# Filling each expected wait of TensorE without a break, and list-scheduling with instruction durations as profiled

## The chip, the cores and the metric

The kernel runs on one core of one Trainium2 chip. The metric is the device time in microseconds (us) of one launch; the time given is a median over runs. Five engines work side by side and each takes its instructions strictly in the order in which they were issued: TensorE (PE: matrix products, and transposes by a product with the identity), VectorE (DVE), ScalarE (ACT), GpSimd (POOL) and SyncE (SP, which issues DMAs). An engine whose next instruction waits for another engine stands still, whatever stands ready behind it. Products land in PSUM; this kernel has eight tiles of 128 x 512 fp32 values there, called banks below (`ps`), and DVE or ACT must read a bank out before it can be used again.

## The reference

The reference is a four-layer decoder on 512 tokens of width 1024, all in fp32. Each layer is a mixer and then a gated feed-forward layer (FFN, hidden width 2816), with RMS norms before each:

```python
def swiglu(x, w_in, w_out):
    gate, up = jnp.split(x @ w_in, 2, axis=-1)
    return (jax.nn.silu(gate) * up) @ w_out
...
    h = x
    for i in range(DEPTH):
        t, j = i % N_MIXERS, i // N_MIXERS
        hn = rmsnorm(h, norm_mix[i])
        if t == 0:
            m = rwkv7_mix(hn, ...)
        elif t == 1:
            m = swa_sink_mix(hn, ...)
        elif t == 2:
            m = sgu_chunk_mix(hn, ...)
        else:
            m = gla_mix(hn, ...)
        h = h + m
        h = h + swiglu(rmsnorm(h, norm_ffn[i]), ffn_w_in[i], ffn_w_out[i])
    return rmsnorm(h, norm_final)
```

The four mixers differ. RWKV-7 is a recurrence over tokens with a 64 x 64 state for each of 16 heads; sliding-window attention (SWA) has sinks and rotary positions; the gated spatial unit (SGU) mixes within chunks of 128 tokens; gated linear attention (GLA) is a recurrence over chunks of 64.

## The kernel before, in words

The kernel is written as a straight program of tile operations. Every operation is first recorded (the recorder is line 233, so nearly every instruction carries that line in the profile), with what it depends on. `Program.run` then is a list scheduler: it keeps a modelled clock for each engine, looks at a window of 700 recorded operations, takes the one that can start first by the model, and issues it. The order that it finds is fixed in the program; the chip only follows it. `Program.price` gives the model's two numbers for each operation: for how long it holds its engine, and how much later its result can be used by another one. For a DVE operation on n elements these are 68 + 1.042 n ns and 130 ns; for ACT 50 or 92 + 0.833 n ns and 150 ns.

Dense projections are done as three products of split operands (high and low parts, in the format fp32r), 512 columns each; the FFN uses a seven-product scheme whose weight combinations are added up by DMAs that POOL issues. ACT makes the high part of each weight tile (`whi<-wraw`), DVE the low part (`wlo<-wraw,whi`). The RWKV mixer is computed in chunks of 64 tokens: per group of four heads a preparation (`rwkv_prepare`, `rwkv_products`, `rwkv_inverse`, tiles `et`, `qk`, `pa`, `pr`, `mt`, `iv`) and then the chain over the chunks (`rwkv_chain`, tiles `wu`, `vu`, `st`, `tok`). Its products are small (64 or 128 columns) and depend on each other by way of DVE, ACT and POOL. An fp32 product of 128 columns appears in the trace as two records, a transpose or an fp32r product as one.

The scheduler also keeps TensorE at work while it has nothing to do. `K.__init__` records a product of the 128 x 128 identity (`ident`) with itself into a bank that nobody reads: line 453 in the profile of this kernel. Whenever TensorE's next operation starts later than the engine is free, `run` calls `keep_warm`. The kernel before divides time into stretches of half of 3413 ns (`PARTS`) and issues such unread products in each stretch only until a goal of work is reached (`LEVEL` x `BUSY` columns over the whole 3413 ns); the rest of the wait stays empty. An unread product takes the bank that has been free for longest, as any other would (`pool.slots["ps"].free`), and if the bank's last user was TensorE itself, the built product waits for TensorE's own semaphore.

Of the kernel before, what the change touches and what calls it, by code (L numbers as in the profile page):

```python
# [17 lines left out]
P = 128  # L18
# [8 lines left out]
PARTS = ((4, 5), (0, 1), (2, 3))  # L27
# [10 lines left out]
class View:  # L38
# [3 lines left out]
    def __init__(self, buf, dims, p0, lo, steps):  # L42
        self.buf, self.dims, self.p0, self.lo, self.steps = buf, dims, p0, lo, steps
# [146 lines left out]
class Program:  # L190
# [2 lines left out]


    WINDOW, SLACK, SEM = 700, 60.0, 100.0
    FREE, LEVEL, MARGIN, PARTS = 4, 1.0, 300.0, 2
    TICK, BUSY = 10240 / 3, 3350.0

    def __init__(self, tc):
        self.tc, self.ops, self.last = tc, [], None  # L200
        nc = tc.nc
        self.tensor, self.vector, self.scalar = Engine(self, "PE", nc.tensor), Engine(self, "DVE", nc.vector), Engine(self, "ACT", nc.scalar)
        self.gpsimd, self.sync = Engine(self, "POOL", nc.gpsimd), Engine(self, "SP", nc.sync)
        self.cold, self.warm, self.fills = 0.0, None, 0

    def pool(self, name, bufs, **kw):
        return Pool(self, name, bufs, kw)
# [54 lines left out]
    def price(self, eng, what, args, kw):  # L262

        views = [a for a in list(args) + list(kw.values()) if isinstance(a, View)]
        n = max(v.free() for v in views)
        columns = sum(v.free() == 1 and v is not views[0] and n > 1 for v in views)
        if what == "dma_start":
            return (490.0 if eng == "SP" else 1000.0), 2000.0
        if eng == "PE":
            if what == "transpose":  # L270
                return 109.0, 200.0
            m, n = args[1].free(), args[2].free()
            if args[2].dtype == F32R:
                return max(n * 0.4167 + 13.5, m * 0.83), 200.0
            return max(n * 1.667 + 5.0, m * 1.667, 340.0 if n < 16 and m == P else 0.0), 200.0
        if eng == "DVE":
            if what == "memset":
                return n * 1.05, 130.0
            fast = what in ("tensor_copy", "tensor_scalar") and not any(v.buf.psum for v in views)
            return 68.0 + n * (0.52 if fast else 1.042) + 61.0 * columns, 130.0  # L280
        if eng == "ACT":
            return (50.0 if any(v.buf.psum for v in views[1:]) else 92.0) + n * 0.833 + 94.0 * columns, 150.0
        if what == "tensor_copy":
            return 36.0 + n * 3.66, 130.0
        return 37.0 + n * (0.83 if len(views) < 3 else 2.8 if views[0].dims[-1][0] < 32 else 2.32), 130.0

    def run(self):
        ops, n = self.ops, len(self.ops)
# [10 lines left out]
        self.work, self.near = work, {}  # L299
        avail = {e: [] for e in now}  # L300
        head, limit = 0, 0
        order = 0
        while order < n:
# [8 lines left out]
            for e, lst in avail.items():  # L312
                cand, floor = None, None
                for i, op in lst:
                    s = max(now[e], op.ready)
                    ok = True
                    for b in op.bufs:
# [6 lines left out]
                        s = max(s, min(sl.free) + self.SEM)  # L324
# [18 lines left out]
            s, i, op, e = best  # L343
# [7 lines left out]
            cost = op.cost  # L351
            if e == "PE":
                tick = int(s // self.TICK)
                if work.get(tick - 1, 0.0) < self.BUSY:
                    self.cold += cost
                    cost *= 2
                self.count(work, self.TICK, s, cost, op.columns)
                self.count(self.near, self.TICK / self.PARTS, s, cost, op.columns)
            end = s + cost
            now[e] = end  # L360
            fin = end + op.lat
# [29 lines left out]
    def keep_warm(self, now, s, work):  # L391

        pool, call, first = self.warm
        t, free = max(now, s - 2 * self.TICK), pool.slots["ps"].free
        span = self.TICK / self.PARTS
        goal = self.LEVEL * self.BUSY / self.PARTS
        while first.done and free and min(free) + self.SEM <= t:
            n = int(t // span)  # L400
            done, end = self.near.get(n, 0.0), (n + 1) * span
            c = 218.0 if work.get(int(t // self.TICK) - 1, 0.0) >= self.BUSY else 436.0
            left = (end - t) / c * 512.0 - (goal - done)
# [10 lines left out]
            self.count(self.near, span, t, c, 512.0)  # L414
            t += c
            if t > s:
                return t
        return now

    def count(self, work, span, t, cost, columns):  # L420
        n = int(t // span)
# [1359 lines left out]
```

## Time and profile before

| | |
|---|---|
| median of three runs | 2632.45 us (2628.38 to 2634.78) |
| the profiled execution's own time | 2641.05 us |
| its span, first to last instruction | 2639.3 us |
| TensorE busy | 2554.7 us, 97%, 12974 records |
| DVE, ACT, POOL busy | 1853.8, 1331.6, 466.0 us |
| unread products, records in the trace | 320 (160 products) |
| mean granted TensorE clock | 0.982 |

The order of the stages in the span: the RWKV mixer up to about 575 us (its first projections up to about 150), then FFN 0, SWA (about 900 to 1100), FFN 1, SGU (about 1425 to 1725), FFN 2, GLA (about 2050 to 2300) and FFN 3. A busy TensorE need not be at its peak: products overlap in the pipeline, their ends are modelled, and gaps shorter than the last product's tail don't show as idle time.

### The profile page before, as it was taken

The numbers are of one execution on the slowest core, as the hardware profiler recorded it, in microseconds if no ns is written. First come the engines' busy times: TensorE is split into PE (matmuls) and PEld (weight loads), VectorE is DVE, ScalarE is ACT, GpSimd is POOL, SyncE is SP. The second block draws the span as 40 slices with busy tenths as digits, with TensorE's granted clock in tenths as the row PEclk, the third lists the DMA queues.
The fourth block names the chain that finished last, engine by engine and source line by source line (L and its number), as shares of the span: only waits on it lengthen the run. The fifth ranks groups of instructions, "written<-read, shape, count | busy, mean of one in ns | idle before, by whom it ended". The sixth has DMA issues, their size and how long they took to land.

```text
span 2639.3 us, 34990 instructions
## 1 busy us (share of the span) xinstructions
PE 2554.7 (97%) x12974; PEld 2083.4 (79%) x12974; DVE 1853.8 (70%) x2888; ACT 1331.6 (50%) x2208; POOL 466.0 (18%) x492
## 2 busy tenths in 40 slices
PE   8999889999999999999999999999999999999998
PEld 7667767889888775888787888898878777888886
DVE  8675777568787966676868474478777735577868
ACT  3544343356555655655555342365645633555545
POOL 1013333311212234121112000012121000012111
PEclk8989989999999999999999999999999999999999
DMA  3220001148988622499896222379897321389885
GB/s 126 72 68 9 7 7 37 39 126 219 226 215 213 178 84 50 101 223 229 208 227 185 96 96 88 80 176 224 211 228 170 119 96 50 81 221 223 209 209 125
DMA packets 127146, 366.24 MB, mean 139 GB/s; under 512 B 13424, under 2 KB 20976, under 8 KB 126976
## 3 DMA queue, kind: packets, MB, share of 16 engines
q0 software_dynamic: 41472, 138.43, 29.1%
q1 hardware_dynamic: 85504, 225.59, 25.3%
q8 instruction: 102, 1.67, 0.3%
q14 instruction: 68, 0.56, 0.1%
HBM read 359.51 MB, written 2.10 MB: 137 GB/s over the span
## 4 chain that ended last, share of the span: by engine, by line
PE 47%; DMA 5%; issue 5%; DVE 5%; ACT 2%; POOL 0%; SPq 0%; ACTq 0%; POOLq 0%; DVEq 0%
PE ps L233 47%; DMA wraw<-ffn_o_a 2%; DMA wraw<-ffn_w_b 2%; DVE slot L233 2%; DVE wlo L233 1%; ACT whi L233 1%; DVE left L233 1%; DMA wraw<-ffn_w_a 1%; ACT slot L233 1%; POOL wraw L233 0%; DVE h L233 0%; DVE mx L233 0%; DMA wraw<-ffn_o_b 0%; DMA slot<-sg_b_s 0%; DMA slot<-slot 0%
## 5 line engine op out<-in xcount | busy, mean ns | idle before, releaser
L233 PE MATMUL ps<-whi,slot 128*128 128x512 f32 (+1 forms) x5072 | 1548.3, 383 | 14.1 <-DVE slot L233 10.0
L233 PEld LDWEIGHTS ps<-whi,slot 128*128 128x128 f32 x5072 | 942.3, 188 | 190.2 <-issue 22.7
L233 DVE TENSOR_TENSOR wlo<-wraw,whi 128x1024 fp32r<-128x1024 f32 (+2 forms) x628 | 723.1, 1157 | 421.7 <-ACT whi L233 420.5
L233 ACT CAST whi<-wraw 128x1024 fp32r<-128x1024 f32 (+3 forms) x632 | 626.6, 995 | 695.5 <-PE ps L233 528.5
L233 PE MATMUL ps<-wlo,slot 128*128 128x512 f32 (+1 forms) x2536 | 969.3, 382 | 3.7 <-DVE wlo L233 3.6
L233 PEld LDWEIGHTS ps<-wlo,slot 128*128 128x128 f32 x2536 | 476.6, 188 | 87.4 <-DVE wlo L233 7.5
L233 PE MATMUL ps<-slot,whi 128*128 128x512 f32 (+2 forms) x864 | 275.0, 396 | 1.2 <-ACT slot L233 0.9
L233 POOL DMA_DIRECT2D wraw<-ffn_w_a x128 | 109.5, 857 | 502.7 <-DVE wlo L233 363.0
L233 DVE TENSOR_TENSOR slot<-ps,slot 128x512 f32<-128x512 f32 (+2 forms) x287 | 153.3, 566 | 60.4 <-PE ps L233 45.7
L233 PEld LDWEIGHTS ps<-slot,whi 128*128 128x128 f32 (+2 forms) x864 | 156.7, 184 | 48.6 <-issue 9.1
L233 POOL DMA_DIRECT2D wraw<-ffn_w_b x64 | 54.8, 864 | 744.6 <-DMA wraw<-ffn_w_b 505.8
L233 PE MATMUL ps<-slot,wlo 128*128 128x512 f32 (+2 forms) x432 | 169.7, 393 | 0.3 <-DVE wlo L233 0.3
L233 DVE TENSOR_TENSOR slot<-left,slot 128x512 fp32r<-128x512 f32 (+1 forms) x214 | 138.9, 666 | 34.9 <-ACT slot L233 29.1
L233 DVE TENSOR_TENSOR h<-h,ps 128x512 f32<-128x512 f32 x192 | 126.7, 682 | 26.4 <-PE ps L233 25.9
L233 ACT CAST slot<-left 128x512 fp32r<-128x512 f32 (+1 forms) x214 | 124.1, 606 | 31.8 <-PE ps L233 24.7
L233 POOL DMA_DIRECT2D wraw<-ffn_o_a x64 | 54.7, 854 | 278.4 <-DVE wlo L233 162.5
L233 ACT COPY slot<-ps 128x512 f32<-128x512 f32 (+2 forms) x137 | 76.1, 568 | 52.1 <-PE ps L233 51.8
L233 PEld LDWEIGHTS ps<-slot,wlo 128*128 128x128 f32 (+2 forms) x432 | 79.5, 184 | 21.2 <-DVE wlo L233 2.2
L233 PEld LDWEIGHTS ps<-ident,slot 128*128 128x128 f32 x580 | 68.3, 142 | 34.5 <-issue 9.5
L233 PE MATMUL ps<-ident,slot 128*128 128x128 f32 x580 | 89.6, 277 | 3.3 <-POOL slot L233 2.6
L233 ACT COPY left<-ps 128x512 f32<-128x512 f32 x100 | 50.6, 556 | 63.7 <-PE ps L233 63.7
L233 DVE TENSOR_TENSOR slot<-slot 128x512 fp32r<-128x512 f32 (+9 forms) x93 | 61.5, 666 | 18.5 <-ACT slot L233 17.1
(260 smaller groups left out, 2517.3 us busy)
## 6 DMA issues: line engine op xcount, KB each, us to landing
wraw<-ffn_w_a SPq DMA_DIRECT2D x128, 512.0 KB, 6.6
wraw<-ffn_w_a POOLq DMA_DIRECT2D x128, 512.0 KB, 6.0
wraw<-ffn_o_a SPq DMA_DIRECT2D x64, 512.0 KB, 4.8
wraw<-ffn_o_a POOLq DMA_DIRECT2D x64, 512.0 KB, 7.5
wraw<-ffn_w_b SPq DMA_DIRECT2D x64, 384.0 KB, 3.5
wraw<-ffn_w_b POOLq DMA_DIRECT2D x64, 384.0 KB, 6.5
wraw<-ffn_o_b SPq DMA_DIRECT2D x16, 512.0 KB, 5.5
wraw<-ffn_o_b POOLq DMA_DIRECT2D x16, 512.0 KB, 6.1
```

Of the source, the lines that this page charges most:

```text
L233: op = self.add(eng.name, lambda: getattr(eng.target, what)(*map(real, args), **{k: real(a) for k, a in kw.items()}), *self.price(eng.name ...
```

## The change

Three things change, all in the scheduler; what the kernel computes stays. First, `keep_warm`: where the model expects TensorE to wait for at least `GAP` = 450 ns, unread products are issued one behind the other until the next of them would end later than `TAIL` = 150 ns before the expected end of the wait. There is no goal any more. Second, `price`: the time for which DVE, ACT and POOL are held goes up (DVE 68 to 148 ns + 1.042 n, ACT 50 or 92 to 158 or 195 ns, POOL 36 or 37 to 60 ns), while the delay until the result can be used goes down (130 or 150 to 60 ns), so that the sum of the two hardly moves. A DVE scan now costs 2.1 ns an element in place of 1.042. Third, for TensorE an fp32 product costs 1.72 n in place of 1.667 n, and 0.56 of that where two products on 64 rows each follow each other on the two halves of the array.

```diff
-    FREE, LEVEL, MARGIN, PARTS = 4, 1.0, 300.0, 2
+    FREE, GAP, TAIL = 4, 450.0, 150.0
     TICK, BUSY = 10240 / 3, 3350.0
...
             if args[2].dtype == F32R:
                 return max(n * 0.4167 + 13.5, m * 0.83), 200.0
-            return max(n * 1.667 + 5.0, m * 1.667, 340.0 if n < 16 and m == P else 0.0), 200.0
+            return max(n * 1.72 + 5.0, m * 1.72, 340.0 if n < 16 and m == P else 0.0) * (0.56 if other else 1.0), 200.0
         if eng == "DVE":
...
-            return 68.0 + n * (0.52 if fast else 1.042) + 61.0 * columns, 130.0
+            return 148.0 + n * (0.52 if fast else 2.1 if what == "tensor_tensor_scan" else 1.042) + 61.0 * columns, 60.0
         if eng == "ACT":
-            return (50.0 if any(v.buf.psum for v in views[1:]) else 92.0) + n * 0.833 + 94.0 * columns, 150.0
+            return (158.0 if any(v.buf.psum for v in views[1:]) else 195.0) + n * 0.833 + 94.0 * columns, 60.0
...
     def keep_warm(self, now, s, work):
         pool, call, first = self.warm
-        t, free = max(now, s - 2 * self.TICK), pool.slots["ps"].free
-        span = self.TICK / self.PARTS
-        goal = self.LEVEL * self.BUSY / self.PARTS
-        while first.done and free and min(free) + self.SEM <= t:
...
-            if done > goal:
-                if end + c > s:
-                    break
-                t = end + 1.0
-                continue
-            if t + c > s and not 0.0 <= left < self.MARGIN:
-                break
+        free = pool.slots["ps"].free
+        if not first.done or not free or s - now < self.GAP:
+            return now
+        t = max(now, min(free) + self.SEM)
+        while True:
+            c = 224.0 if work.get(int(t // self.TICK) - 1, 0.0) >= self.BUSY else 448.0
+            if t + c > s - self.TAIL:
+                return now
             call()
...
             t += c
+            now = t
```

The built program holds 568 unread products in place of 160, in 104 groups in place of 61. 395 of them (145 before) stand ahead of FFN 0's first product, 62 of these (35 before) in the first four groups of the program, and 173 (15 before) behind FFN 0's beginning. Twelve groups have 13 products or more and hold 321 together. As the prices differ, the order of all other work moves as well: the lists of TensorE, DVE and ACT differ nearly everywhere in the RWKV mixer, and SP issues some of SWA's copies (`slot<-slot`) later among its weight loads.

TensorE, in the RWKV mixer, where a group's chain over the chunks (`wu`, `vu`) meets the next group's triangular blocks (`mt`, made by DVE and POOL), before:

```order
L233 MATMUL ps<-vu,tok 128x128 x2
L233 MATMUL ps<-vu,pr 64x64 x4
L233 MATMUL ps<-ident,h 128x128 x4
L233 MATMUL ps<-ident,et 128x128 x4
L453 MATMUL ps<-ident 128x128 x10
L233 MATMUL ps<-ident,mt 128x128 x4
L233 MATMUL ps<-mt,z 128x128 x4
L233 MATMUL ps<-st,qk 128x128
```

and now:

```order
L233 MATMUL ps<-vu,tok 128x128 x2
L233 MATMUL ps<-vu,pr 64x64 x4
L233 MATMUL ps<-ident,et 128x128 x4
L233 MATMUL ps<-ident,h 128x128 x4
L444 MATMUL ps<-ident 128x128 x62
L233 MATMUL ps<-ident,mt 128x128 x4
L233 MATMUL ps<-mt,z 128x128 x4
L233 MATMUL ps<-st,qk 128x128 x2
```

The group of ten unread products has become one of 62; the shorter groups that stood in the chain ahead of it are fewer.

TensorE, some 40 rows earlier in the same chain, where a chunk's solve (`wu,iv`) waits for ACT's copy of `wu`, now:

```order
L233 MATMUL ps<-wu,iv 64x64 x4
L233 MATMUL ps<-twa,wa 128x512
L233 MATMUL ps<-vu,pa 64x64 x4
L233 MATMUL ps<-vu,pr 64x64 x4
L444 MATMUL ps<-ident 128x128 x23
L233 MATMUL ps<-wu,iv 64x64 x4
L444 MATMUL ps<-ident 128x128 x2
L233 MATMUL ps<-vu,tok 128x128 x2
```

A group of 23 stands here where no group of that size stood. By the semaphore values in the built program twelve of these 23 turn on one single free bank, so that each waits for the product just ahead of it. Over the whole program that holds for 34 of the 568 (1 of 160 before): 19 in the RWKV mixer and 15 in SWA; another 47 (12 before) wait for the one before that, with two banks to turn on.

TensorE in SWA, between the scores of one group of heads and the transposes of its probabilities, before (the last half of the heads):

```order
L233 MATMUL ps<-slot 128x128 x2
L233 MATMUL ps<-slot 128x256 x11
L233 MATMUL ps<-slot 128x128 x2
L233 MATMUL ps<-slot 128x256 x9
L233 MATMUL ps<-whi,slot 128x512
L233 MATMUL ps<-wlo,slot 128x512
```

and now:

```order
L233 MATMUL ps<-slot 128x256 x7
L444 MATMUL ps<-ident 128x128 x5
L233 MATMUL ps<-slot 128x128 x2
L233 MATMUL ps<-slot 128x256 x11
L444 MATMUL ps<-ident 128x128 x12
L233 MATMUL ps<-ident,slot 128x128 x2
```

Where projection products on `whi` and `wlo` followed the scores, 5 and 12 unread products and then the transposes do.

More of the change, by code (lines that the diff above doesn't have):

```diff
@@ L203, in __init__ @@
         self.gpsimd, self.sync = Engine(self, "POOL", nc.gpsimd), Engine(self, "SP", nc.sync)
-        self.cold, self.warm, self.fills = 0.0, None, 0
+        self.cold, self.warm, self.fills, self.rows = 0.0, None, 0, (P, 0)
     def pool(self, name, bufs, **kw):
@@ L298, in run @@
         dma, table, work = 0.0, None, {}
-        self.work, self.near = work, {}
+        self.work = work
         avail = {e: [] for e in now}
@@ L357, in run @@
                 self.count(work, self.TICK, s, cost, op.columns)
-                self.count(self.near, self.TICK / self.PARTS, s, cost, op.columns)
             end = s + cost
@@ L395, in keep_warm @@
         pool, call, first = self.warm
-        t, free = max(now, s - 2 * self.TICK), pool.slots["ps"].free
-        span = self.TICK / self.PARTS
-        goal = self.LEVEL * self.BUSY / self.PARTS
-        while first.done and free and min(free) + self.SEM <= t:
[L400 to L403, printed above, removed]
-            if done > goal:
-                if end + c > s:
-                    break
-                t = end + 1.0
-                continue
-            if t + c > s and not 0.0 <= left < self.MARGIN:
-                break
+        free = pool.slots["ps"].free
[6 more added lines that the diff above has]
+                return now
             call()
@@ L413, in keep_warm @@
             self.count(work, self.TICK, t, c, 512.0)
-            self.count(self.near, span, t, c, 512.0)
             t += c
-            if t > s:
-                return t
-        return now
+            now = t
     def count(self, work, span, t, cost, columns):
```

9 lines of the change are left out of this document (6 added, 3 removed).

## The prediction

> **What bounds the kernel now.** I read the busy shares first, then TensorE's windows by stage with the granted clock, then who ends its waits. TensorE is the busiest engine:
>
> ```profile
> PE 2554.7 (97%) x12974; PEld 2083.4 (79%) x12974; DVE 1853.8 (70%) x2888; ACT 1331.6 (50%) x2208; POOL 466.0 (18%) x492
> ```
>
> The windows show that two quite different programs lie behind the 97% (stretch; its length, busy time and records of PE, PEld, DVE, ACT, POOL; clock; DMA share; GB/s):
>
> ```profile
> 25.00:150.00 125.00, 124.22 (x512) 88.14 (x513) 97.52 (x153) 68.48 (x104) 7.20 (x4) 1.00 0.24 79
> 150.00:475.00 325.00, 291.67 (x2031) 237.48 (x2029) 236.43 (x446) 134.75 (x280) 108.22 (x102) 0.89 0.07 20
> 475.00:575.00 100.00, 96.56 (x804) 86.18 (x804) 54.49 (x116) 37.90 (x87) 24.27 (x27) 1.00 0.31 98
> 575.00:1100.00 525.00, 513.70 (x2437) 408.68 (x2436) 390.74 (x610) 303.68 (x579) 122.94 (x124) 1.00 0.64 157
> 1100.00:1725.00 625.00, 618.54 (x2924) 516.54 (x2923) 416.05 (x577) 293.90 (x420) 75.24 (x82) 1.00 0.61 158
> 1725.00:2300.00 575.00, 568.82 (x2669) 458.52 (x2669) 381.12 (x598) 297.82 (x472) 62.93 (x75) 1.00 0.61 152
> 2300.00:2639.30 339.30, 324.35 (x1528) 272.04 (x1526) 261.40 (x360) 186.47 (x261) 59.81 (x70) 0.99 0.83 195
> ```
>
> From 575 us on, TensorE sets the pace at full clock: idle 11.3, 6.5 and 6.2 us in the three whole rows, and a few us of the 15 in the last, most of which are the tail behind the last product: some 28 us of 2064. From 150 to 475 us, the core of the RWKV mixer, it stands idle for 33.3 us, the clock averages 0.89, and even the busy time is loose. An unread product's price comes from these rows (start, duration, count of records, two for a product):
>
> ```profile
> 7.05 1.06 PE L453 MATMUL ps<-ident 128*128 128x128 f32 x8
> 281.74 3.99 PE L453 MATMUL ps<-ident 128*128 128x128 f32 x28
> 279.88 0.71 PE L453 MATMUL ps<-ident 128*128 128x128 f32 x4
> 499.40 1.03 PE L453 MATMUL ps<-ident 128*128 128x128 f32 x4
> L453 PE MATMUL ps<-ident x320: 270/275/582, 1.4 to 2622.7; 128*128 128x128 f32 x160
> ```
>
> Eight records in 1.06 us, less the last one's own 0.275, make 0.112 us a record, 0.224 us a product. At that price the 2031 records from 150 to 475 us fill about 227 of 325 us (the longer and the shorter products there about cancel); 98 us are left, of which 33.3 are idle. The half clock explains part of the rest:
>
> ```profile
> 157.10:177.60 20.50, 19.84 (x80) 12.85 (x81) 10.15 (x14) 4.92 (x15) 1.32 (x1) 0.50 0.08 26
> 256.10:269.80 13.70, 13.70 (x70) 10.04 (x68) 8.68 (x14) 3.93 (x12) 0.23 (x1) 0.50 0.03 10
> 293.70:300.50 6.80, 4.77 (x22) 4.77 (x22) 3.26 (x5) 0.39 (x2) 6.10 (x6) 0.50 0.02 4
> 351.70:361.90 10.20, 10.20 (x52) 8.45 (x51) 5.58 (x16) 3.10 (x9) 2.51 (x4) 0.50 0.04 13
> 375.60:389.20 13.60, 11.78 (x59) 10.41 (x60) 7.95 (x19) 4.51 (x7) 7.41 (x9) 0.50 0.06 10
> 433.60:437.00 3.40, 3.40 (x18) 2.97 (x18) 3.16 (x13) 1.69 (x5) 0.53 (x2) 0.50 0.81 271
> 457.50:460.90 3.40, 3.40 (x19) 3.06 (x18) 3.05 (x7) 0.00 (x0) 1.58 (x2) 0.50 0.07 20
> ```
>
> These seven stretches, 71.6 us, ran at half clock throughout, with 320 records. TensorE is busy for 67.1 of the 71.6 us, so there it paces itself.
>
> **The change part by part.** *The clock.* What comes ahead of a half-clock stretch is a stretch with little work:
>
> ```profile
> 153.70:157.10 3.40, 0.34 (x2) 0.00 (x0) 3.40 (x6) 2.48 (x3) 3.29 (x2) 1.00 0.19 70
> 348.30:351.70 3.40, 1.03 (x12) 0.89 (x12) 3.19 (x12) 0.37 (x2) 0.45 (x1) 1.00 0.00 0
> 430.20:433.60 3.40, 2.54 (x24) 2.13 (x25) 3.23 (x9) 0.49 (x2) 3.05 (x3) 1.00 0.12 22
> ```
>
> Groups of up to 62 products in the expected waits leave hardly such a stretch. Run at full clock, 320 records need 320 x 0.112 = 35.8 us less; that is the upper bound. The lower one is 0: TensorE is then only sooner at the next wait. I take 22 us, some 60% of it: the busy share speaks for nearly all, DVE at 41.8 of the 71.6 us in the same rows for less. **-22 us.**
>
> The Trainium skill (TensorE: Matmul & The Clock Gate, "Why this matters for your kernels") says that only idle gaps over about 3 us between bursts bring the half clock back. The trace agrees at 153.7 and not at 430.2 us, where TensorE shows 2.54 of 3.4 us busy and the clock is halved all the same. By that rule the 92 short groups (247 products) would buy no clock.
>
> *The products in the RWKV mixer.* 395 in place of 145 stand ahead of FFN 0: 250 x 0.224 = 56 us of TensorE time. The 98 us between 150 and 475 us can hold them, if each stands in a real wait. Two things make them longer than their waits. First, the bank: where two products in a row must take the same bank, two cost 1.03 in place of 0.71 us (the pair at 499.40 is the one such case, the pair at 279.88 an ordinary one), so 0.32 us for each that waits for the one ahead: 19 of them here, 6 us. With two banks to turn on, the run at 281.74 gives (3.99 - 0.28) / 13.5 = 0.275 us a product; 0.05 us for a few dozen is 2 us and left out. Second, DVE's new price is its duration in the profile, but durations overlap:
>
> ```profile
> 1407.70 1.27 DVE L233 TENSOR_TENSOR h<-h,ps 128x512 f32<-128x512 f32 x2
> 1408.29 0.68 DVE L233 TENSOR_TENSOR h<-h,ps 128x512 f32<-128x512 f32 x1
> ```
>
> The second starts 0.59 us after the first, which lasts 0.68. So the list now expects DVE's queue 0.08 us too late for each instruction that doesn't depend on the one before. The six long groups in this stretch (54, 23, 62, 42, 15, 14) are about 47 us of wait; at 446 DVE instructions in 325 us, 64 of them run meanwhile, and 64 x 0.08 = 5 us of products would come after the operand is there. Together **+11 us**; bounds 0 (DVE is as late as expected) and 6 + 446 x 0.08 = +42 us (each DVE instruction on the path).
>
> The Trainium skill (Perfetto Trace Analysis, "Optimizing Scalar/DVE Operations") gives about 60 ns of overhead for a DVE operation on SBUF and 93 for ScalarE as busy time, and about twice that as profiled latency, since the end overlaps the next instruction. The pair at 1407.70 agrees, and the old prices (68, 92 ns) are of that kind; by this rule alone the upper bound just given would be the nearer one.
>
> *The order.* Other new prices come nearer to the trace, and these operations decide when TensorE is served from 150 to 475 us (a DVE group by form; three of PE's waits there, with total, times and longest; two DVE instructions in order of time):
>
> ```profile
> L233 DVE TENSOR_TENSOR_SCAN ew<-keep,ew 128x512 f32<-128x512 f32 x6 | 9.6, 1605 | 10.9 <-ACT ew L233 10.9
> PE ps L233 <- DVE mt L233: 8.4, 3, 4.4
> PE ps L233 <- DVE et L233: 7.3, 4, 3.5
> PE ps L233 <- POOL mt L233: 3.9, 4, 2.5
> 281.63 1.23 DVE L233 TENSOR_TENSOR rs_t<-grs 128x8 f32<-128x8 f32 x1
> 286.47 0.12 DVE L233 TENSOR_TENSOR rs_t<-grs 128x8 f32<-128x8 f32 x1
> ```
>
> The scan was priced at 68 + 512 x 1.042 = 601 ns and takes 1605; the same operation on eight elements takes 0.12 us at 286.47 and 1.23 us at 281.63. A list that takes DVE for slower puts TensorE's other ready work ahead of such a result. I take **-10 us**, half of the 19.6 us in the three waits; bounds -20 (all of it) and +10, as a new order can also put the chain later.
>
> *Behind FFN 0's beginning* 173 in place of 15 products, 158 x 0.224 = 35 us, and 15 x 0.32 = 5 us for SWA's groups on one bank. There is 28 us of idle time; most of it lies where such groups stand (block starts, the ends of FFNs, SWA's score groups), and a DMA that comes late absorbs others, as here in FFN 1 (start, us):
>
> ```profile
> 1297.35 7.62 DMA wraw<-ffn_o_a
> 1305.07 1.06 ACT whi L233
> 1307.29 0.69 DVE h L233
> ```
>
> Until 1308.12 TensorE waits for this chain, so products that delay it ahead of it cost nothing. I let 29 of the 40 us fall into waits: **+11 us**; bounds 0 and +40. ACT, DVE and POOL have the same work as before here. SP's queue is moved too (a few SWA copies now go out behind weight loads), at a DMA share of 0.64 in the row from 575 us: I take nothing for it. Behind unread products that last too long stands the next projection, and DVE then waits for that one's bank.
>
> The first four groups grow by 27 products, inside the wait for the first DMA and the first norm: nothing.
>
> *Sum:* -22 + 11 - 10 + 11 = -10 us on the profiled 2641.05 us, 2631; that execution lies 8.6 us above the median of the runs, 2632.45, so **2622 us**.
>
> **The rivals.** *The fillers outlast their waits* (slower). Place: the stages behind 575 us, where idle time is 1.4% of the span, and the long RWKV groups. DVE and ACT are ready before the padded prices say so, the products run on in order, and the next product stands behind them. Price: clock -22, RWKV +11, no gain from the order, +35 behind 575 us: +24, 2657 us. It decides once more than some 32 us (clock plus order) of the 96 us of added products fall on ready work. For it: the pair at 1407.70. Against it: the DVE instructions that take 1.2 us for eight elements.
>
> *The chain bounds the mixer* (no change). DVE, POOL and ACT set the RWKV stage; a full clock makes the waits longer, the products fill them, and the later stages give and take alike: 0, 2632 us. For it: the three waits above. Against it: 67.1 of 71.6 us busy at half clock.
>
> *The order itself is better* (a larger gain): clock -36, order -20, products 11, nothing lost behind 575 us: -45, 2587 us.
>
> *The change doesn't keep the clock*: a wait that the list doesn't foresee stays empty. Then the clock's 22 us are halved, +1 us in all, which goes with no change.
>
> **How the numbers follow.** A difference under 0.3% (8 us) can't be told from none here. Forecast 0.38 (its own range 2606 to 2632: 0.30 faster, 0.08 same); fillers too long 0.30 (0.27 slower, 0.03 same); chain 0.20 (0.03, 0.14, 0.03); order 0.12 (faster). Together faster 0.45, same 0.25, slower 0.30. The range takes in the slower rival's 2657 and leaves out most of the large gain: 2596 to 2658.
>
> **What would show it.** Right: the clock at 1.00 in the windows from 150 to 475 us; that stage, by its programs' names, shorter by some 20 us; TensorE busier, 60 us or more of idle gone. Wrong on the products: the stretch from FFN 0 to the end longer by 25 us or more, and DVE standing idle for TensorE where groups of seven or eight stand. Wrong on the bank: the 23 products of the RWKV chain spaced by 0.22 us, not partly by 0.55. Wrong on the clock: rows at 0.50 in that stage.

## The result

The changed kernel takes 2672.58 us (median of four runs, 2671.08 to 2678.28) against 2630.41 us of the kernel before in the runs beside it: 1.0167 times, 95% interval 1.0139 to 1.0194. It is slower by 42 us, where 2622 us were forecast, and it lies outside the range.

The profile after, in the same two views as before: the busy shares, and the windows by stage (shifted by some 15 us from FFN 0 on, as the stages are).

```profile
PE 2624.5 (98%) x13790; PEld 2168.7 (81%) x13790; DVE 1873.1 (70%) x2888; ACT 1337.0 (50%) x2208; POOL 469.2 (18%) x492
25.00:150.00 125.00, 124.40 (x520) 89.43 (x519) 99.00 (x153) 66.17 (x101) 6.84 (x4) 1.00 0.25 82
150.00:475.00 325.00, 309.79 (x2357) 258.65 (x2355) 229.44 (x426) 133.89 (x274) 103.15 (x93) 0.97 0.06 19
475.00:590.00 115.00, 112.16 (x941) 100.95 (x941) 64.42 (x137) 44.42 (x106) 31.75 (x36) 1.00 0.27 83
590.00:1115.00 525.00, 519.01 (x2474) 415.77 (x2473) 384.49 (x585) 291.90 (x545) 122.78 (x124) 0.99 0.64 157
1115.00:1740.00 625.00, 623.76 (x2984) 526.30 (x2983) 423.37 (x584) 297.65 (x424) 76.45 (x82) 1.00 0.61 158
```

Read the row from 150 to 475 us against the one of before. The clock has risen from 0.89 to 0.97, and TensorE's idle time has fallen from 33.3 to 15.2 us: what the change was built to do happened. But DVE has done 426 instructions by 475 us where it had done 446, ACT 274 in place of 280. TensorE has 326 more records there. Its unread products alone have gone from 150 records to 508, so of all its other work it has done less. Their rows (the first is of before, the other two of the changed kernel; length, busy time and records of PE and PEld):

```profile
150.00:475.00 325.00, 27.26 (x150) 21.69 (x150) 0.89 0.07 20
...
150.00:475.00 325.00, 69.27 (x508) 61.48 (x508) 0.97 0.06 19
590.00:1115.00 525.00, 26.58 (x146) 22.21 (x146) 0.99 0.64 157
```

TensorE is busier, and the mixer is behind. Where the time went shows when each of TensorE's instructions is matched with the same one of the other trace, by the place at which the program records it. The start of four such instructions, before, and the difference to it (us):

| | before | after | E2 | E5 | E12 | E13 | E18 | E19 |
|---|---|---|---|---|---|---|---|---|
| FFN 0 begun | 619.0 | +14.0 | -23.8 | +15.3 | +9.1 | +17.9 | +1.0 | -18.6 |
| ahead of SWA's projections | 906.6 | +13.2 | -18.5 | +16.0 | +9.7 | +16.4 | +0.2 | -17.9 |
| behind SWA's scores | 1093.5 | +26.3 | -18.3 | +29.0 | +24.6 | +25.9 | +16.7 | -1.0 |
| ahead of the tail | 2611.0 | +28.3 | -19.7 | +31.9 | +24.2 | +30.2 | +19.3 | -0.3 |

(The columns E are experiments below.) The change loses 14 us up to FFN 0 and 13 us in SWA, and next to nothing in the 1500 us behind. The profiled execution of before lies some 9 us above the median of its runs, that of the changed kernel at its median; so these differences come to less than the 42 us of the medians, and the lead that the column E2 shows over before is larger than that of the medians.

### The profile page after: what moved, and what is told of

It is laid out like the page before. It is cut to its first block, busy times and chain, and to the rows that moved or that the text cites. A ratio compares the mean times of both kernels' runs of the same rounds, so it can differ in the third digit from the quotient of the medians.

```text
span 2671.2 us, 36661 instructions
## 1 busy us (share of the span) xinstructions
PE 2624.5 (98%) x13790; PEld 2168.7 (81%) x13790; DVE 1873.1 (70%) x2888; ACT 1337.0 (50%) x2208; POOL 469.2 (18%) x492
## 4 chain that ended last, share of the span: by engine, by line
PE 58%; DVE 2%; DMA 1%; issue 1%; ACT 1%; POOL 0%; SPq 0%; ACTq 0%; DVEq 0%; POOLq 0%
PE ps L233 57%; PE ps L444 1%; DVE slot L233 1%; DMA wraw<-ffn_w_a 1%; ACT whi L233 1%; DMA wraw<-ffn_o_a 0%; DVE wlo L233 0%; ACT slot L233 0%; DVE mx L233 0%; DVE h L233 0%; POOL wraw L233 0%; SPq L233 0%; DMA slot<-slot 0%; DVE rs_t L233 0%; DVE left L233 0%
## 5 line engine op out<-in xcount | busy, mean ns | idle before, releaser
L233 DVE TENSOR_TENSOR wlo<-wraw,whi 128x1024 fp32r<-128x1024 f32 (+2 forms) x628 | 720.4, 1158 | 404.9 <-ACT whi L233 394.4
L233 ACT CAST whi<-wraw 128x1024 fp32r<-128x1024 f32 (+2 forms) x632 | 625.7, 993 | 723.2 <-PE ps L233 571.8
L444 PE MATMUL ps<-ident 128*128 128x128 f32 x1136 | 165.2, 290 | 8.1 <-DVE bonus L233 2.5
L444 PEld LDWEIGHTS ps<-ident 128*128 128x128 f32 x1136 | 149.0, 197 | 22.9 <-PE ps L444 8.8
L233 DVE TENSOR_TENSOR slot<-left,slot 128x512 fp32r<-128x512 f32 x214 | 134.7, 650 | 13.0 <-ACT slot L233 9.5
L233 ACT CAST slot<-left 128x512 fp32r<-128x512 f32 (+1 forms) x214 | 120.0, 594 | 20.6 <-PE ps L233 18.3
```

The costliest lines, as they stand in the source:

```text
L233: op = self.add(eng.name, lambda: getattr(eng.target, what)(*map(real, args), **{k: real(a) for k, a in kw.items()}), *self.price(eng.name ...
L444: self.nc.tensor.target.matmul(self.ps.tile_pool.tile([P, S], F32, name="ps")[:, :P], self.ident.real(), self.ident.real(), start=True, st ...
```

## The experiments

### The filling rule and the prices, each alone

E1 is the kernel before with the new `price` and the old `keep_warm`; E2 the changed kernel with the old `price`:

```diff
E1:  def price(...):        # as after
     def keep_warm(...):    # as before
E2:  def price(...):        # as before
     def keep_warm(...):    # as after
```

> The kernel before with the new prices alone; unread products still by the old rule (312 in place of 160, of the change's 568). If the longer holding prices make the order itself worse (theory O: waits of TensorE get longer and the products only fill them), this takes most of the change's +42 us: 2655 to 2675 us. If the products that outlast their waits are the cause (theory F), 152 more products at 0.224 us are at most +34 us and, at the change's ratio of 42 us to 408 products, some +16 us: 2640 to 2650 us. Prediction's own term for the order (-10 us) would give 2620 us.

> The change with the old prices: waits are filled without a break, but as the old prices expect them (206 unread products). Theory O: no new order beyond what 46 more products move, the half clock partly gone: 2615 to 2632 us. Theory F: the rule of filling itself costs, so above the kernel before, 2636 us or more.

E1: 2670.56 us, 1.0173 (1.0156 to 1.0190). E2: 2619.74 us, 0.9972 (0.9959 to 0.9986), faster than before. The two rows of E2 from 150 us on:

```profile
150.00:475.00 325.00, 297.06 (x2271) 245.50 (x2269) 242.44 (x460) 142.20 (x299) 112.44 (x107) 0.96 0.08 25
475.00:575.00 100.00, 97.47 (x737) 87.57 (x736) 66.48 (x145) 51.11 (x111) 25.25 (x28) 1.00 0.38 99
```

With the filling rule alone the clock is at 0.96 too, and DVE has done 460 instructions by 475 us, 34 more than in the changed kernel. So the filling rule does what it is for, and the prices alone lose more than it brings: 53 us lie between E2 and the changed kernel. With the new prices the filling rule brings next to nothing: E1, which has the old rule and 312 unread products, takes 2670.56 us, the changed kernel with 568 takes 2672.58.

### The unread products in the changed order

E5 keeps the changed kernel's order and leaves out every unread product after the first 62; the list still plans them.

```diff
-            call()
+            if self.fills < 62:
+                call()
             self.fills += 1
```

> The changed kernel with its order of all other instructions, but none of the unread products issued after the first 62 (the list plans them, and so keeps the order, and they are left out when the instructions are written). Theory T (the order makes the waits longer; the products sit in these waits): the waits stay and TensorE falls to half clock in them and behind them, so not faster than 2665 us. Rival P (the products run past the arrival of the next operand and are themselves the loss): faster than the changed kernel by what they overran, 2650 us or less.

2674.39 us, 1.0171 (1.0138 to 1.0204), the same as with them.

```profile
150.00:475.00 325.00, 259.28 (x1836) 209.81 (x1835) 228.80 (x425) 133.54 (x273) 102.50 (x93) 0.87 0.06 19
```

A mean of 0.87 out of full and half clock is 325 x 0.13 / 0.5 = 85 us at half clock; 0.97 is 20 us. Yet DVE is at 425 instructions at 475 us without the products, against 426 with them. E5 changes two things at once, which could cancel: a product that ran too long no longer holds anything up, and the clock falls. The traces leave little room for that. DVE's 2888 instructions stand in the same order in both, and from 150 to 475 us the same instruction starts between 2.6 us earlier and 1.7 us later than with the products (medians over 10 us); in the whole trace no instruction is more than 5.6 us off. The largest gain lies behind a group of 23 products, where a product of the chain on `wu,iv` waits for ACT's copy of `wu` (the copy and the product in the changed kernel, then the product in E5):

```profile
L233 ACT COPY wu<-ps x1: 368/368/368, 333.0 to 333.0; 64x256 f32<-64x256 f32 x1
337.51 0.67 PE L233 MATMUL ps<-wu,iv 64*64 64x64 f32 x8
...
331.20 1.11 PE L233 MATMUL ps<-wu,iv 64*64 64x64 f32 x8 [5.20 <-ACT wu L233]
```

In the changed kernel the copy is done at 333.4 us and the product starts 4.1 us later: here the unread products do outlast their wait. In E5 it starts 6.3 us earlier; three chunks on, at 357 us, 0.4 us are left of that. All such gains up to 475 us add up to some 4 us, the losses to some 6. So in this order 508 records of products and 65 us of half clock cost some 4 and 6 us in the mixer, and neither sets its pace. The loss of 53 us is not, but for a few us, that products run on ready work; it is in the order.

That doesn't make half clock free in general. The executions of one and the same kernel differ, and time and clock go together. E5's four took 2666.09 us at a mean clock of 0.979, 2674.36 and 2674.41 at 0.974 and 0.975, and 2677.43 at 0.973. Of 63 executions of the kernel before, the three at 0.982 took 2638.61 to 2641.05 us, the 25 at 0.989 took 2620.35 to 2629.99. There 37 us more of half clock (2630 x 0.007 / 0.5) go with some 13 us more of time. Only one execution of each kernel has a trace, so where those 37 us lie isn't known.

E4 asks for the banks instead: it fills no wait with fewer than three banks free, so that fewer products wait for the one ahead of them.

```diff
-        if not first.done or not free or s - now < self.GAP:
+        if not first.done or len(free) < 3 or s - now < self.GAP:
```

> The change, but unread products only while the list counts at least three free banks (478 in place of 568). If the turning on one or two banks is the cause (theory B), 34 products at 0.32 us and 47 at 0.05 us go, 13 us, with what they hold up in SWA up to 20: 2652 to 2660 us. Theory F counts the 90 products too: about 2655 us. Theory O: SWA and the mixer keep their new order, 2662 to 2673 us.

2679.94 us, 1.0204 (1.0180 to 1.0228): no faster, with DVE's order nearly the changed kernel's (114 of 2888 places differ). The bank's price itself is in the changed kernel as it was read beforehand (a group of 23 and one of five in the timeline: start, duration, records):

```profile
328.11 9.47 PE L444 MATMUL ps<-ident 128*128 128x128 f32 x46
973.58 2.67 PE L444 MATMUL ps<-ident 128*128 128x128 f32 x10 [0.19 <-DVE slot L233]
```

Five products take 2.67 us, where ten records at 0.112 us, the last at 0.275, make 1.28: some 0.35 us more for each of the four that wait for the one ahead, against 0.32 read beforehand. And this is how long TensorE's weight load stood idle ahead of the products of line 444 until TensorE was done (total us, times):

```profile
  PE ps L444: 8.8, 34
```

It waited for the product ahead 34 times, 0.26 us of idle time each, as many times as the built program has one-bank products. E4 does not rid the mixer of them: 14 such waits are left there, nine of them in a stretch at half clock, where such a product takes 0.85 us. They belong to the group between ACT's `wu` and the product on `wu,iv`: the copy is done at 340.5 us in E4, the product starts at 350.9, DVE falls from 7 to 13 us behind the changed kernel there, and that isn't made up. So unread products can cost time in the mixer. In SWA E4 has no such wait, and it loses 16 us there all the same.

### Which price

All of these are E2 (old prices) with some of the new ones put in, but for E3, which is the changed kernel with some of the old ones back:

```diff
E7:  TensorE's new prices only (1.72 n, 0.56 for the two halves)
E8:  the scan's 2.1 n and GpSimd's new prices only
E6:  DVE -68.0 +148.0, -130.0 +60.0; ACT -50.0/92.0 +158.0/195.0, -150.0 +60.0
E9:  DVE -68.0 +70.0; ACT -50.0/92.0/150.0 +52.0/94.0/152.0
E3:  changed kernel; DVE 148.0 -> 68.0, 60.0 -> 130.0; ACT 158.0/195.0 -> 50.0/92.0, 60.0 -> 150.0
```

> The change with one part undone: DVE and ACT are again priced at the time from one start to the next (68, 50, 92 ns and 130, 150 ns), while TensorE's new prices, the scan's and POOL's stay (294 unread products). Theory O with the holding price as its cause: back to 2632 us or below, 2610 to 2632. If TensorE's or POOL's new prices were the cause, it stays at 2655 or above. Theory F: 274 fewer products than the change, some 28 us less: about 2645 us.

> Filling rule of the change, old prices but for one part: DVE and ACT hold their engine for their profiled duration (553 unread products). Measured so far against the kernel before: the filling rule with all old prices 0.9972, the whole change 1.0167. If the holding price is the cause (theory O): most of the way to the change, 2655 to 2675 us. If the list is merely sensitive to any change of its numbers (theory L: the old numbers give a lucky order): between 2620 and 2660, no telling.

> Filling rule of the change, old prices but for TensorE's (1.72 n and 0.56 for pairs on 64 rows; 212 unread products). These come nearer to the trace (0.112 us a record of 128 columns), and the order moves little (1173 lines of difference in TensorE's list). Theory O: 2610 to 2626, as with the filling rule alone. Theory L: anywhere up to 2645.

> Filling rule of the change, old prices but for the scan's and POOL's (286 unread products). Undoing DVE's and ACT's holding price in the change left 1.0085, so 22 us stay unexplained. If these prices are that rest: 2635 to 2650. If TensorE's prices or a mixture are: 2615 to 2630.

> Filling rule of the change, old prices with 2 ns added to each DVE and ACT operation's hold: a change that means nothing on the chip (226 unread products). Theory O: like the filling rule alone, 2612 to 2628. Theory L: 10 us or more away from it, 2630 or above, since 4350 lines of TensorE's list differ.

E7: 2620.96 us, 0.9976 (0.9958 to 0.9993), as E2. E9: 2622.43 us, 0.9976 (0.9951 to 1.0001): two nanoseconds do nothing, so the order isn't a matter of chance at every step. E8: 2640.22 us, 1.0040 (1.0021 to 1.0060). E6: 2700.03 us, 1.0256 (1.0229 to 1.0283), 80 us over E2. E3: 2649.80 us, 1.0085 (1.0065 to 1.0104). DVE's and ACT's pair of numbers is the larger part, scan and GpSimd a smaller one; they don't add up (the changed kernel has both and is faster than E6).

E10 and E11 split E6 by engine, E15 takes the new latencies only:

```diff
E10: E2 with DVE -68.0 +148.0, -130.0 +60.0
E11: E2 with ACT -50.0/92.0 +158.0/195.0, -150.0 +60.0
E15: E2 with the latencies only: DVE -130.0 +60.0, ACT -150.0 +60.0
```

> The filling rule with the old prices and only VectorE's new fixed price (148 ns of occupation and 60 of latency in place of 68 and 130). Theory M (the list takes VectorE for 80 ns per independent instruction slower than it runs): VectorE is the busiest engine behind TensorE in the mixer, so most of the 80 us that both prices cost come back: 2650 to 2700 us. If ScalarE's price were the cause: about 2620 us.

> The filling rule with the old prices and only ScalarE's new fixed price (158 and 195 ns of occupation in place of 50 and 92, latency 60 in place of 150). Theory M with VectorE as the place: 2615 to 2645 us. If ScalarE's price is the cause: 2680 us or more.

> The filling rule with the old prices and only the new latency of 60 ns on VectorE and ScalarE, with the old occupations. Theory T: the tie alone makes the chains run in blocks, 2650 us or more. Rival H: occupations are the old ones, few products are emitted, about 2620 us.

E10: 2698.38 us, 1.0275 (1.0249 to 1.0301). E11: 2648.40 us, 1.0085 (1.0067 to 1.0104). So it is VectorE: its price alone costs as much as both, 79 us over E2, and ScalarE's alone costs 29. E15: 2719.04 us, 1.0346 (1.0315 to 1.0376), the slowest of all, 99 us over E2: the new latencies without the new occupations are worse than the two together. So E10 doesn't say which of VectorE's two numbers did it. E14 was to have the new occupations with the old latencies, but by a slip in its edit ScalarE's latency stood at 1158 ns, not 150; it took 2706.45 us, and tells nothing of the question; the new occupations alone were not run.

> The filling rule with the old prices (2619.7 us) and only the new fixed occupations of VectorE (148 in place of 68 ns) and ScalarE (158 and 195 in place of 50 and 92), with the old latencies of 130 and 150 ns: a dependent step is now dearer than before by 80 and 108 ns, an independent one too. Theory T: the latency still exceeds the 60 ns of slack, so chains stay interleaved: 2615 to 2640 us. Rival H: as slow as with both prices (2700 us) or nearly, 2655 us or more.

### How wrong the new prices are, and whether that is the cause

Over the trace of E2, of VectorE's instructions that don't depend on the one just ahead, the median one starts 82 ns before that one ends (2552 pairs); of those that do, 34 ns after its end (335 pairs). On ScalarE, half of the instructions start before the one ahead ends, the median one of these by about 100 ns. From start to start the old occupations, 68 + 1.042 n ns, are right within 2 ns for the median pair on VectorE; the new ones are 80 ns too long for each independent instruction, and right within 17 ns for a dependent step. If the size of that error were the cause, half of it should cost part of the time, and a small error the other way little:

```diff
E16: E2 with DVE 108.0 and 95.0, ACT 104.0/143.5 and 105.0    (half way)
E12: E2 with DVE 48.0 and 150.0, ACT 30.0/72.0 and 170.0      (20 ns too short)
```

> The filling rule with prices half way: VectorE 108 ns of occupation and 95 of latency, ScalarE 104 and 143.5 and a latency of 105. Theory M: the loss grows with the error, so between 2619.7 and 2700: 2635 to 2680 us. Theory F: no relation, the time may lie at either end or beyond.

> The filling rule with occupations 20 ns shorter than the old ones (VectorE 48 in place of 68, ScalarE 30 and 72 in place of 50 and 92) and latencies 20 ns longer, so that a dependent step costs the same. Theory M: the error is a quarter of the new prices', in the other direction: within some 15 us of the old prices' 2619.7, so 2610 to 2635 us. Theory F (any other order loses as much): 2645 us or more.

E16: 2627.66 us, 1.0006 (0.9993 to 1.0020). E12: 2664.25 us, 1.0151 (1.0133 to 1.0168). Half of the error costs 8 us of the 80, and a quarter of it in the other direction 45. So the error does not act by its size, though two points are few. What the slow orders have in common had to be looked for in the traces.

### What the slow orders have in common

The RWKV mixer has a state chain for each of four groups of heads (`rwkv_chain`): eight chunks one behind the other, each a few small products with copies on ACT (`wu`, `vu`) and the state's update on DVE (`st<-ps,st`) between them. While the third group's chain runs, the fourth group's triangular inverse (`rwkv_inverse`) is computed: a run of 30 dependent DVE instructions on `et`, then products on `mt` and the result `iv`. The timeline of the changed kernel where the two meet (rows of PE and DVE in order of time; start, duration; `...` for rows left out):

```profile
430.91 1.06 PE L233 MATMUL ps<-vu,tok 128*128 128x128 f32 x4
...
433.47 0.16 DVE L233 TENSOR_TENSOR et<-et 128x2 f32<-128x2 f32 x1
433.66 0.16 DVE L233 TENSOR_REDUCE et<-et 128x2 f32<-128x2 f32 x1
...
436.06 8.43 PE L444 MATMUL ps<-ident 128*128 128x128 f32 x74
...
443.71 0.62 DVE L233 TENSOR_REDUCE et<-et 128x30 f32<-128x450 f32 x1
444.25 0.41 DVE L233 TENSOR_TENSOR st<-ps,st 128x256 f32<-128x256 f32 x1
...
444.72 1.38 PE L444 MATMUL ps<-ident 128*128 128x128 f32 x10 [0.23 <-DVE st L233]
...
445.94 0.61 PE L233 MATMUL ps<-st,h 128*128 128x128 f32 x4
```

The update's operand, the products on `vu,tok`, is done at 432.0 us. The update itself starts at 444.25, behind all 30 steps on `et`, and 37 unread products fill the wait on TensorE (the row with 74 records). The next product of the chain starts at 445.94. The same place in E2:

```profile
405.29 0.71 PE L233 MATMUL ps<-vu,tok 128*128 128x128 f32 x4 [0.34 <-ACT vu L233]
...
408.46 0.16 DVE L233 TENSOR_TENSOR et<-et 128x2 f32<-128x2 f32 x1
...
409.15 0.15 DVE L233 TENSOR_REDUCE et<-et 128x2 f32<-128x2 f32 x1
409.21 0.41 DVE L233 TENSOR_TENSOR st<-ps,st 128x256 f32<-128x256 f32 x1
409.54 1.05 DVE L233 TENSOR_TENSOR et<-et 128x8 f32<-128x8 f32 x1
409.77 0.68 PE L233 MATMUL ps<-st,h 128*128 128x128 f32 x4 [0.73 <-DVE st L233]
```

Here the update goes between two steps on `et`, 3.2 us after its operand. The list makes the difference: it lets an instruction pass an earlier recorded one only where it can start more than `SLACK` = 60 ns sooner. A dependent step is ready at the end of the one before plus the latency, 130 ns of old. At the new 60 ns nothing is more than 60 ns sooner, so the whole run on `et` goes out as one block. E13 changes that by one nanosecond (latencies of DVE, ACT and GpSimd):

```diff
-    ... + 61.0 * columns, 60.0
+    ... + 61.0 * columns, 61.0
```

> The changed kernel with the latency of VectorE, ScalarE and GpSimd instructions at 61 ns instead of 60. The list lets an independent instruction overtake an earlier recorded one only if it can start more than SLACK = 60 ns sooner; a dependent instruction of the same engine can start at the end of the one before plus the latency. At 60 nothing independent can get between two dependent steps, at 61 it can, as it could at 130 and 150. Theory T (this tie makes the list run dependent chains of VectorE as one block, and what TensorE waits for comes later): most of the 42 us go, 2615 to 2640 us. Rival H (the longer occupation, 148 ns in place of 68 on VectorE, makes the list believe longer waits and fill them): one nanosecond changes nothing of that, 2655 us or more.

2678.37 us, 1.0189 (1.0158 to 1.0220): no gain. But the block is gone, and the trace shows what took its place (E13's timeline):

```profile
423.40 0.21 DVE L233 TENSOR_TENSOR et<-et 128x50 f32<-128x50 f32 x1
423.53 0.42 DVE L233 TENSOR_TENSOR st<-ps,st 128x256 f32<-128x256 f32 x1
423.86 0.20 DVE L233 TENSOR_REDUCE et<-et 128x10 f32<-128x50 f32 x1
...
480.99 1.06 PE L233 MATMUL ps<-mt 128*128 128x128 f32 x8
481.98 0.67 PE L233 MATMUL ps<-wu,iv 64*64 64x64 f32 x8
482.08 0.69 DVE L233 TENSOR_TENSOR iv<-mt,ps 128x512 f32<-128x512 f32 x1 [1.52 <-PE ps L233]
```

and its instructions on `wu` from 412 to 483 us (count, min/median/max ns, first and last start):

```profile
L233 ACT COPY wu<-ps x4: 366/368/368, 412.1 to 432.2; 64x256 f32<-64x256 f32 x4
```

The update now goes between the steps on `et`. But ACT writes the fourth chunk's `wu` at 432.2 us, and the product that reads it stands at 481.98, 49 us later, right behind the inverse's last product on `mt`. It waits for nothing that the chip computes. Followed through the list's own decisions it is held back there by the rule that hands out PSUM banks (`Slots.may`): with two banks free, the banks held by or planned for what is recorded ahead of it, the inverse above all, come to seven of eight, one more than the rule lets pass, and the chain's bank is given out only when the inverse no longer needs its own. E12 and E8 have the same; here is E12, from its `wu` row and its timeline:

```profile
L233 ACT COPY wu<-ps x3: 365/365/367, 415.8 to 428.0; 64x256 f32<-64x256 f32 x3
```

```profile
475.80 1.06 PE L233 MATMUL ps<-mt 128*128 128x128 f32 x8
476.79 0.68 PE L233 MATMUL ps<-wu,iv 64*64 64x64 f32 x8
```

So there are two ways in which the inverse holds the chain up. The third group's chain, from the starts of the same instructions in each trace (us): its first chunk's first product, the second's, the fourth chunk's product on `wu,iv`; then the inverse's last `iv` on DVE, and the mixer's last `out<-out,ps`:

| | chunk 1 | chunk 2 | chunk 4 | last `iv` | last `out` | time, us |
|---|---|---|---|---|---|---|
| before | 418.9 | 431.0 | 445.5 | 483.5 | 554.2 | 2630 |
| E2 | 397.8 | 409.8 | 424.0 | 457.3 | 530.9 | 2619.7 |
| E7 | 394.5 | 399.6 | 416.5 | 459.3 | 526.5 | 2621.0 |
| E16 | 398.9 | 407.3 | 420.7 | 459.0 | 523.0 | 2627.7 |
| E11 | 409.5 | 418.0 | 432.2 | 468.4 | 536.1 | 2648.4 |
| after | 423.0 | 445.9 | 474.9 | 476.5 | 560.4 | 2672.6 |
| E13 | 411.4 | 415.1 | 482.0 | 482.1 | 566.5 | 2678.4 |
| E12 | 403.8 | 414.4 | 476.8 | 476.9 | 560.3 | 2664.3 |
| E3 | 404.2 | 412.3 | 472.6 | 472.8 | 559.0 | 2649.8 |
| E8 | 408.5 | 417.1 | 477.3 | 477.4 | 564.4 | 2640.2 |
| E10 | 421.2 | 461.0 | 491.3 | 487.4 | 580.1 | 2698.4 |
| E15 | 448.7 | 472.7 | 505.5 | 505.6 | 594.1 | 2719.0 |

In the fast orders chunk 4 starts 33 us and more ahead of the last `iv`; in the slow ones with it or behind it, but for E11, which has its chain in time and loses elsewhere (some 10 us of it in SWA, against E2). The chain's place alone doesn't order the times: E8 has it as late as E12 and is 24 us faster. At FFN 0 the two are within 2 us of each other; but E8 loses 1 us in SWA, where E12 loses 15.

### Letting the chain go first

Two runs test whether that place is the cause. In both, the instructions of the chains of all four groups count as recorded 300 places earlier when the list chooses; all else stays. E18 is the changed kernel with this edit, E19 is E12 with it.

```diff
...
+        op.key = op.i - self.ahead
...
-                    bisect.insort(avail[op.eng], (op.i, op))
+                    bisect.insort(avail[op.eng], (op.key, op))
...
         for b in range(NB):
+            nc.ahead = 300.5
...
+            nc.ahead = 0.0
             if b % 2:
                 self.rwkv_out(sb, b // 2, y, tg)
```

> The changed kernel with all of its prices and its filling rule, and one edit in the list's order: the instructions of the state chain of the RWKV mixer count as recorded 300 places earlier, so that they go ahead of the block inverse and the products where both are ready. Theory C (the prices cost time because they push the state chain, which is serial from chunk to chunk, behind the block inverse): some 20 to 30 us of the mixer come back, 2640 to 2655 us, and the loss in the attention stage stays. Rival (where the chain stands is only a companion of another cause): 2665 us or more.

> The filling rule with the short occupations (2664.3 us without this edit), and the state chain of the mixer counting as recorded 300 places earlier. Theory C: the chain no longer waits 49 us for a PSUM bank behind the inverse, 2610 to 2640 us. Rival: 2655 us or more.

E19: 2641.11 us, 1.0054 (1.0038 to 1.0070), 23 us less than E12; chunk 4 starts at 419.4 us, the last `out` at 537.7 in place of 560.3. For those 23 us of the 45 that E12 loses the chain's place is the cause; most of the rest is SWA. E18: 2662.95 us, 1.0138 (1.0119 to 1.0156), 10 us less than the changed kernel, between what the two theories gave. The chain is free: chunk 4 at 433.8, the last `out` at 538.4 in place of 560.4. But the inverse's last `iv` moves from 476.5 to 489.7 us, and by the table of stages only 13 of the 22 us arrive at FFN 0. And as the edit moves the chains of the earlier groups too, the third group's begins at 414.4 in place of 423.0 us: part of the 13 was won ahead of the place shown above.

## Why the prediction failed

**The step that failed is the order: -10 us, with bounds of -20 and +10.** Between E2 and the changed kernel, which differ by the prices alone, it is +53 us: by the starts of the same instructions 38 up to FFN 0, 45 behind SWA and 48 ahead of the tail. The working put the overlap of 0.08 us on VectorE, which it had read correctly from one pair of rows, to nothing but products that last too long (64 x 0.08 = 5 us). The new numbers' effect is on the order: with VectorE's alone E10 lost 79 us over E2. The working expected a gain from the other new prices, the scan's above all, because they come nearer to the trace. E8 has the scan's and GpSimd's new prices alone, and it is 20 us slower than E2: a price nearer to the trace made no better order. And the working looked at three waits of before for what an order may gain or lose, 19.6 us in all. A wait's length in the old order is no bound for a new one: one place in the list can move a chain by 50 us, as in E12.

**The clock, -22 us: the half clock went as forecast, its worth did not follow.** By the mean clock, half clock between 150 and 475 us fell from 325 x 0.11 / 0.5 = 72 us to 26 in E2, and to 20 in the changed kernel. In E2 that comes with a lead of 24 us at FFN 0, but over the profiled execution of before, which at a clock of 0.982 is the slowest of the 63 on record; by the medians E2 gains 7 us. The sum of the prediction takes that execution's half clock off with the 22 us and then once more the 8.6 us by which it lies above its median, which, to judge by the executions of before, are in good part the same time; without that it would have been 2631 us. In the changed order the clock was worth a few us at the most, as E5 shows. What sets the pace there is the order of the work on the other engines, of which E18 and E19 show the chain to be a part. So the rival *the chain bounds the mixer* comes nearest to the changed kernel, but with the chain itself made longer; as a forecast of no change it was wrong.

**The products in the RWKV mixer, +11 us: they hold the chain up in places, and the stage is no shorter without them.** With 508 of their records in the stage or with none of them the time is the same. The price of the one-bank products, 0.32 us, was right in size (0.35 us for the five of SWA) and in number (34). Behind the group of 23, twelve of them, 3.8 us, do hold the chain up by 4.1 us, as the working had it; but what the chain wins there without them it doesn't keep (E5). This is also where the slower rival fails. That its 2657 us lie nearest to the result is luck: by its own terms the time without the products and with the half clock back (E5) is 2657 - 11 - 35 + 22 = 2633 us, and it is 2674.4.

**Behind FFN 0, +11 us: right in size by luck, wrong in cause.** The changed kernel loses 14 us there, 13 of them in SWA. E5 loses 17 there with hardly a product left, so that is the order again, not the 40 us of products. In SWA the projections of the next heads come later against the scores, and unread products stand in their stead, as the order printed with the change shows; which decision of the list puts them there wasn't tried. E12, E18 and E19 lose 15 to 17 us at the same place, and so does E4 (16), which has no one-bank product there.

**What stays open.** Of the 53 us between E2 and the changed kernel, putting the state chains first gives back 10 (E18). SWA holds 13. Most of the rest lies in the mixer ahead of the third group's chain, which begins at 423.0 in place of 397.8 us (448.7 in E15, 414.4 in E18), and I have no run that takes that apart. That the new prices cause the loss is shown (E1, E2, E10); that they do so by being wrong is not, as E12 and E15 lose 45 and 99 us with other errors.

## What to carry to other kernels

The time from start to start of back-to-back instructions and the duration of a profile row are not the same: on VectorE they differ by 82 ns here. The fastest kernels here have tables that follow the first to within some 2 ns on VectorE (E2, E7, E9), and the one "as measured" by durations, with its shorter latency, was the dearest part of this change (E10). But the time is no smooth function of the prices (E12, E16), so each table needs its run. A price moves the order by way of ties and thresholds, so an equal latency and slack, or one bank too few, can set a serial chain behind work that is needed only later; look for an instruction whose operand is long there (`wu` at 432.2, its product at 481.98) before you look at the sum of waits. A change with two parts is best tried part by part: the filling rule alone (E2, 0.9972) is better than both kernels.

## What the runs showed of the hardware

What half clock costs depends on the order: in the changed one, 85 against 20 us of it between 150 and 475 us left the starts of VectorE's instructions within some 3 us (E5 and the changed kernel), but over the 63 executions of the kernel before, a mean clock of 0.982 in place of 0.989 goes with some 13 us more.
